# A hybrid attention, retention and pooling backbone: retention in its own queue, pooling in place, and a reordered opening

## The chip, the cores and the metric

The kernel runs on one core of a Trainium2 chip. Its time is the device time of one execution in microseconds; the profile is one execution of its own. PE is the matrix engine (TensorE), DVE the VectorE, ACT the ScalarE, POOL the GpSimd, and SP the SyncE, which here issues DMAs. Each engine works through its own instructions in the order in which the program wrote them, and semaphores hold an instruction back until what it needs is there.

## The reference

Two layers run over 256 latent tokens and 256 context tokens of width 1024, all in float32. The second layer carries the latent tokens on alone; its context tokens only give keys and values.

- Every layer: `u = modulate(rmsnorm(h)) @ w_in`, split into the inputs of three mixers and three gates. The modulation is `silu(c) @ w_ada + b_ada` (adaLN).
- Neighbourhood attention (8 heads of 64): latent queries see a window of the 4 x 64 grid with a bias, and all context keys, in one softmax; context queries see the context.
- Retention (4 heads, keys of 64, values of 128), both directions: `o = ((q k^T) * decay) v`, then a normalization of every head over its 128 values, times `silu(g) * gn_g`.
- Pooling: four groups of 128 channels with windows of 2, 4, 8 and 16 tokens: `(mean over the window - u) @ pool_w * pool_scale`.
- Merge: `(sig(ga)*(a@wpa) + sig(gb)*(r@wpb) + sig(gc)*(p@wpc)) @ w_out`, a gated residual, then a second modulated norm, SwiGLU of hidden width 2816, and a gated residual. A final RMSNorm ends it.

## The kernel before

Every product of float32 operands is made of three matmuls: operands are split into a rounded high part and the rest (`hi`, `lo`), and PE adds `wh*xh + wl*xh + wh*xl` in one PSUM bank (`mm3`, L194 to L198). Activations lie with channels on the partitions and tokens (512, or 256 latent ones) along the row. Weights stream from HBM in 276 chunks of 128 x 1024 (`raw`), and ACT and DVE split each into `hl` (L124, L113) up to three chunks ahead of its use.

PSUM has eight banks under four tags: `pg` (4, products of the projections), `pS` (2, scores), `pT` (1, transposes) and `pO` (1). A tile of a tag waits until the bank that was freed first has been read.

`start()` is the opening. It loads the vectors (`vec`) and the eight tiles of h, computes the norm of h (eight squares into `sq`, summed into `acc`, then summed over partitions by L499, the reciprocal root by `norm_rstd`, and a broadcast by L290), spreads silu(c) over all partitions (L480 on PE, `spread`, L483, copies it into `cb`), and makes the first modulation from adaLN weights in their natural layout: `nat_first` (L459, sixteen matmuls of a chunk `wn`), `nat_copy` and `nat_second` (L469). Its loop over eight chunks then makes seven of the first eight key and query products; the weights of the eighth are kept in `w7` and used behind the loop (L548). Its tiles lie in a pool of their own (`st`), which is closed at its end; the pool of the first mixer (`mx0`) then takes the same place.

`mixer(l, ...)` is the attention, retention and pooling of one layer (L568 to L1052). The order of PE's work around the change is written out in its last part (L829 to L855 and L1035 to L1052): keys and queries, the token-major V (`tokmajor`, CV), retention keys, retention queries, pooling inputs u, the token-major retention values (CRV), the gate products (CG), then the branches A (attention), C (pooling) and B (retention). A branch has four pairs of output chunks; each pair takes two gate products, whose sigmoid (L1000) frees their banks, and two branch products.

The small work of the mixers is woven into these products by lanes. A lane is a list of Python generators; each `next` emits a few instructions and yields. `tick()` (L153) advances the first generator of each of the lanes `pool`, `rope` and `attn` by one step; a generator that is exhausted leaves the list at its next step. `fm` calls `tick` for every two block products of 512 columns or four of 256, and `tokmajor` for every two of 512. `drain(name)` runs what is left of a lane at once. On every second tick DVE's part of the weight splits and, by a rate, adaLN sums (`ada_units`, L385) are emitted too. `pipeline(items, stride)` runs items of several stages staggered, two ticks a stage: first what runs on ACT, DVE and POOL, then PE's part.

The attention's lane has 16 latent items (and 8 context ones in layer 0), one after the other by one stage. The retention's generators are put into the same lane after the gate products: `ret_stack` splits its keys and queries (`rkd`, `rkl`, `rqs`), `ret_item` makes the decay tables of a head (L897 to L906), scores, product with v (L941) and statistics, and `ret_fin` normalizes (L970), transposes (L977) and multiplies by the gate (L980). The decay tables of head 0 are emitted ahead of them, and the four Silu of the gates (L1044) behind. `drain("attn")` ahead of branch B runs what is left.

`pool_task` is the pooling's lane: for each of the four groups POOL adds shifted rows (L803) and corrects the borders (L812), four steps pass, DVE subtracts (L820) into a tile `pl` of the tag `t2`, which it shares with the attention's probabilities, four more steps later PE multiplies (L780) into a `pg` bank, and one step later ACT writes the scaled result over u (L784). `st["hold"]` is 1 while `tokmajor(CRV)` holds all four `pg` banks; the subtractions wait for its end.

Of the kernel before, what the change touches and what calls it, by code (L numbers as in the profile page):

```python
# [8 lines left out]
F32 = mybir.dt.float32  # L9
# [9 lines left out]
KT = 8  # L19
# [13 lines left out]
def hybrid_dit_kernel(ctx: ExitStack, tc: tile.TileContext, hT, wst, adaf, adan, vec_d,  # L33
# [52 lines left out]
        return vec[:, l * V_L + off + i:l * V_L + off + i + 1]  # L86

    raw_t, hl_t = {}, {}
    st = {"dma": 0, "prep": 0, "half": 0, "credit": 0.0, "rate": 0.0, "cap": 10 ** 6, "hold": 0, "lazy": False}
    total = 2 * NCH  # L90

    def raw_tile():
# [46 lines left out]
        load_to(i + 5)  # L139
        flush()  # L140

    lanes = {"attn": [], "pool": [], "rope": []}
    ada_q = []

    def step(q):
        while q:
            try:
                next(q[0])
                break
            except StopIteration:  # L150
                q.pop(0)

    def tick():  # L153
        step(lanes["pool"])
        step(lanes["rope"])
        step(lanes["attn"])
        if st["half"] == 0:
            prep_lo()
            st["credit"] += st["rate"]
            while ada_q and st["credit"] >= 1:  # L160
                ada_q.pop(0)()
                st["credit"] -= 1
        st["half"] ^= 1
# [195 lines left out]
    def new_acc():  # L359
        return sm.tile([128, 512], F32, name="acc", tag="acc", bufs=1)  # L360
# [62 lines left out]

    def start():
        with tc.tile_pool(name="st", bufs=1) as sp:
            nc.scalar.dma_start(out=vec, in_=vec_d)
            h_tiles()
            P.memset(ones, 1.0)
            P.memset(eps, 1e-6)
            make_identity(nc, ident)  # L430
            csil = sp.tile([128, 8, 32], F32, name="csil")
            P.memset(csil, 0.0)
            S.activation(tiny(1, "dummy"), eps, AF.Silu)

            acc = new_acc()
# [5 lines left out]
            st["w7"] = w7 = sp.tile([128, 2, 8, 128], F32R, name="w7")  # L441
            wn = {}

            def nat_load(k):
                if k < KT:
                    wn[k] = sp.tile([128, 8, 256], F32, name="wn", tag="wn", bufs=3)
                    nc.sync.dma_start(out=wn[k], in_=adan[k])

            for k in range(3):
                nat_load(k)  # L450
                load_to(k)

            outs = [pg() for _ in range(4)] + [pS(), pS(), pT(), pO()]
            nat = outs[7]

# [26 lines left out]
            def spread(i):  # L482
                S.copy(cb[i // 2][:, (i % 2) * 512:(i % 2) * 512 + 512], outs[i])  # L483

            for k in range(KT):
                t = sp.tile([128, 512], F32, name="sq", tag="sq", bufs=4)
                if k in (2, 5):
                    V.tensor_tensor(t, h[k], h[k], op=ALU.mult)
                else:
                    S.activation(t, h[k], AF.Square)  # L490
                if k == 0:
                    V.tensor_copy(acc, t)
                else:
# [12 lines left out]
            Rs = sp.tile([128, 512], F32, name="Rs")  # L506
# [61 lines left out]
    def mixer(l, mp, outs, u):  # L568
# [204 lines left out]
        def pool_task():  # L773
            pw = sm.tile([128, 4, 128], F32, name="pw", tag="acc", bufs=1)
            nc.sync.dma_start(out=pw, in_=pw_d[l])
            late = {}

            def pmm(gi, o2):
                pp = pg()
                TE.matmul(pp[:, :nq], pw[:, gi], o2[:, :nq], start=True, stop=True)  # L780
                return pp

            def pev(gi, pp):
                S.activation(up[gi][:, :, 8:264], pp[:, :nq].rearrange("p (s t) -> p s t", t=256), AF.Copy,  # L784
                             scale=vcol(l, V_PS, gi))

            t = [0]

            def pause():
                t[0] += 1  # L790
                if t[0] in late:
                    gi, o2 = late.pop(t[0])
                    pp = pmm(gi, o2)
                    late[-t[0] - 1] = (gi, pp)
                elif -t[0] in late:
                    pev(*late.pop(-t[0]))

            for gi in range(4):
                b = mp.tile([128, 1 + so, 272], F32, name="pb", tag="pb", bufs=1)
                a, w = up[gi], 1  # L800
                for j in range(gi + 1):
                    n = 272 - 2 * w + 1
                    P.tensor_tensor(b[:, :, :n], a[:, :, :n], a[:, :, w:w + n], op=ALU.add)  # L803
                    a = b
                    w *= 2
                    yield
                    pause()
                s0 = 8 - w // 2
# [13 lines left out]
                late[t[0] + 4] = (gi, o2)  # L822
                yield
                pause()
            while late:
                yield
                pause()

        if both:  # L829
            for i in range(8):  # L830
                if i == 4:
                    prep_to(10)
                (ev_nak(i) if i < 4 else ev_naq(i - 4))(outs[i])
        else:
            for i, o in enumerate(outs):
                ev_nak(i)(o)
            n = len(outs)
            fm([(chunk8(base + CK + i), ev_nak(i)) for i in range(n, 4)], hn, ALL)
            fm([(chunk8(base + CQ + i), ev_naq(i)) for i in range(4)], hn, cq)
        if both:  # L840
            decay_logs(u)
        st["lazy"] = True
        lanes["attn"].append(pipeline(items, 1, (10 if both else 0)))
        tokmajor(base + CV, hn, nav)
        fm([(chunk8(base + CRK + i), ev_k(i)) for i in range(2)], hn, ALL)
        fm([(chunk8(base + CRQ + i), ev_q(i)) for i in range(2)], hn, cq)
        fm([(chunk8(base + CU + i), ev_u(i)) for i in range(4)], hn, cq)
        drain("rope")
        lanes["pool"].append(pool_task())
        st["hold"] = 1  # L850
        tokmajor(base + CRV, hn, rv)
        st["hold"] = 0
        fm([(chunk8(base + CG + i), ev_g(i)) for i in range(4)], hn, cq)
        drain("attn")
        st["lazy"] = False  # L855

        m = [mp.tile([128, 512], F32, name=f"m{i}", tag=f"nak{i}") for i in range(4)] + nav
# [106 lines left out]
        def ret_fin(hd):  # L964
# [17 lines left out]

            return [(None, None), (norm, None), (None, trans), (fin, None)]

        def msplit(ks):
            for k in ks:
                split([t[:, cq] for t in hn[k]], m[k][:, cl])
# [60 lines left out]
        drain("attn")  # L1048
        branch(base + CB, [gt[i] for i in range(4)], False, True)
        if both:  # L1050
            h_tiles()
# [298 lines left out]
```

## Time and profile before

| | us |
|---|---|
| median of 3 runs | 1366.77 |
| fastest and slowest run | 1366.04, 1368.06 |
| the profiled execution | 1367.57 |
| span of the profiled execution, first to last instruction | 1365.8 |
| PE busy | 1326.2 |
| PE loading weights | 1151.9 |
| DVE busy | 847.6 |
| ACT busy | 580.7 |
| POOL busy | 152.7 |

The mean granted clock of PE in the span was 0.987 of full speed. A busy time says how long an engine had an instruction at work; matmuls overlap at their ends, so PE's is not the time that its multiplications need. L12 is line 12 of the kernel as printed. A wait is the idle time of an engine ahead of an instruction, put down to what released it last. A row of a timeline gives the start in us from the start of the span, the duration, the engine, line and operation, what is written and read, the shape, a count of merged instructions and, in brackets, the idle time ahead.

### The profile page before, as it was taken

The numbers are of one execution on the slowest core, as the hardware profiler recorded it, in microseconds if no ns is written. First come the engines' busy times: TensorE is split into PE (matmuls) and PEld (weight loads), VectorE is DVE, ScalarE is ACT, GpSimd is POOL, SyncE is SP. The second block draws the span as 40 slices with busy tenths as digits, with TensorE's granted clock in tenths as the row PEclk, the third lists the DMA queues.
The fourth block names the chain that finished last, engine by engine and source line by source line (L and its number), as shares of the span: only waits on it lengthen the run. The fifth ranks groups of instructions, "written<-read, shape, count | busy, mean of one in ns | idle before, by whom it ended". The sixth has DMA issues, their size and how long they took to land.

```text
span 1365.8 us, 20012 instructions
## 1 busy us (share of the span) xinstructions
PE 1326.2 (97%) x7842; PEld 1151.9 (84%) x7842; DVE 847.6 (62%) x1454; ACT 580.7 (43%) x907; POOL 152.7 (11%) x213
## 2 busy tenths in 40 slices
PE   7999999899999999999999999999999999999997
PEld 5777777788888898888888888988889999899997
DVE  4566452877877666566565654676438877655554
ACT  4455555452232444232123232456466545643453
POOL 0034113211000010000000000232134200000000
PEclk8999999999999999999999999999999999999998
DMA  8433312343544514454445652143336665455552
GB/s 301 164 99 132 104 63 92 124 137 126 169 170 163 192 62 154 139 170 158 149 140 186 212 171 87 61 159 108 131 124 197 223 239 185 140 185 198 181 176 95
DMA packets 61150, 207.28 MB, mean 152 GB/s; under 512 B 6912, under 2 KB 11392, under 8 KB 60032
## 3 DMA queue, kind: packets, MB, share of 16 engines
q1 hardware_dynamic: 49392, 163.96, 35.8%
q10 hardware_dynamic: 11664, 42.04, 9.1%
q8 instruction: 62, 1.02, 0.3%
q14 instruction: 32, 0.26, 0.1%
HBM read 204.93 MB, written 1.05 MB: 151 GB/s over the span
## 4 chain that ended last, share of the span: by engine, by line
PE 89%; DVE 6%; ACT 3%; issue 1%; DMA 1%; POOL 0%; DVEq 0%; ACTq 0%; SPq 0%; POOLq 0%
PE pg L196 26%; PE pg L197 26%; PE pg L198 26%; PE po L941 1%; PE po L687 1%; PE pt L675 1%; DVE hl L113 1%; PE po L459 1%; PE ps L643 1%; PE ps L644 1%; DVE nakl L628 1%; DMA bm<-in_bias 1%; DVE rkl L876 0%; DVE naq L638 0%; DVE acc L494 0%
## 5 line engine op out<-in xcount | busy, mean ns | idle before, releaser
L196 PE MATMUL pg<-hh,hl 128*128 128x256 f32 (+1 forms) x1568 | 528.1, 337 | 2.5 <-ACT tmp L1000 1.4
L197 PE MATMUL pg<-hh,hl 128*128 128x256 f32 (+1 forms) x1568 | 522.9, 333 | 1.4 <-DVE hl L113 1.4
L198 PE MATMUL pg<-hl,hl 128*128 128x256 f32 (+1 forms) x1568 | 523.3, 334 | 0.6 <-POOL hl L326 0.5
L113 DVE TENSOR_TENSOR hl<-raw,hl 128x1024 fp32r<-128x1024 f32 (+1 forms) x276 | 341.4, 1241 | 172.2 <-ACT hl L124 166.9
L124 ACT CAST hl<-raw 128x1024 fp32r<-128x1024 f32 (+1 forms) x276 | 286.9, 1043 | 211.4 <-PE pg L198 112.3
L196 PEld LDWEIGHTS pg<-hh,hl 128*128 128x128 f32 x1568 | 299.7, 191 | 36.1 <-issue 3.8
L197 PEld LDWEIGHTS pg<-hh,hl 128*128 128x128 f32 x1568 | 299.6, 191 | 31.1 <-DVE hl L113 2.1
L198 PEld LDWEIGHTS pg<-hl,hl 128*128 128x128 f32 x1568 | 299.2, 191 | 30.6 <-POOL hl L326 1.4
L385 DVE CUSTOM_DVE_ANT_0 tmp<-ada,cb 128x1024 bf16<-128x1024 f32 x128 | 156.1, 1226 | 26.7 <-DMA ada<-in_adaf 17.3
L196 PE MATMUL pg<-fh,hl 128*128 128x256 f32 (+1 forms) x374 | 121.6, 325 | 0.0
L197 PE MATMUL pg<-fh,hl 128*128 128x256 f32 (+1 forms) x374 | 121.4, 325 | 0.0
L198 PE MATMUL pg<-fl,hl 128*128 128x256 f32 (+1 forms) x374 | 121.4, 325 | 0.0
L326 POOL TENSOR_TENSOR hl<-tmp,hh 128x256 fp32r<-128x256 f32 x20 | 14.8, 739 | 626.3 <-ACT hh L315 371.1
L298 ACT CAST fh<-sg 128x512 fp32r<-128x512 f32 (+1 forms) x44 | 22.6, 513 | 141.0 <-DVE sg L1150 141.0
L196 PEld LDWEIGHTS pg<-fh,hl 128*128 128x128 f32 x374 | 70.1, 187 | 7.2
L198 PEld LDWEIGHTS pg<-fl,hl 128*128 128x128 f32 x374 | 70.1, 187 | 7.2
L197 PEld LDWEIGHTS pg<-fh,hl 128*128 128x128 f32 x374 | 70.1, 188 | 7.1
L342 DVE SCALAR_TENSOR_TENSOR h<-pg,mods,h 128x256 f32<-128x256 f32 x72 | 32.7, 479 | 65.6 <-PE pg L198 65.4
L1150 DVE TENSOR_TENSOR sg<-pg,sg 128x512 f32<-128x512 f32 (+1 forms) x44 | 24.5, 556 | 51.2 <-PE pg L198 47.8
L1000 ACT ACTIVATE tmp<-pg 128x512 f32<-128x512 f32 (+1 forms) x48 | 23.5, 490 | 76.4 <-PE pg L198 75.2
L196 PE MATMUL pg<-hl,hh 128*128 128x512 f32 x128 | 50.8, 397 | 1.7 <-DVE nakl L628 1.7
L1147 ACT ACTIVATE sg<-pg 128x512 f32<-128x512 f32 (+1 forms) x44 | 21.6, 490 | 68.4 <-PE pg L198 68.4
(248 smaller groups left out, 1555.7 us busy)
## 6 DMA issues: line engine op xcount, KB each, us to landing
raw<-in_wst SPq DMA_DIRECT2D x276, 512.0 KB, 3.8
ada<-in_adaf ACTq DMA_DIRECT2D x80, 512.0 KB, 4.2
wn<-in_adan SPq DMA_DIRECT2D x8, 1024.0 KB, 7.4
h<-in_hT SPq DMA_DIRECT2D x16, 256.0 KB, 5.5
bm<-in_bias SPq DMA_DIRECT2D x32, 128.0 KB, 2.1
out<-yt SPq DMA_DIRECT2D x4, 256.0 KB, 3.2
cs<-in_rope SPq DMA_DIRECT2D x2, 256.0 KB, 3.1
pw<-in_pw SPq DMA_DIRECT2D x2, 256.0 KB, 3.8
```

Of the source, the lines that this page charges most:

```text
L113: V.tensor_tensor(a[:, 1], r[:, b], a[:, 0].bitcast(F32), op=ALU.subtract)
L124: S.copy(a[:, 0], r[:, b])
L196: TE.matmul(o, wh, xh, start=a, stop=False)
L197: TE.matmul(o, wl, xh, start=False, stop=False)
L198: TE.matmul(o, wh, xl, start=False, stop=z)
L298: S.copy(d0, src)
L326: P.tensor_tensor(hn[k][1][:, c], t[:, c], hi, op=ALU.subtract)
L342: V.scalar_tensor_tensor(h[k][:, c], o, mods[l][:, col + k, s:s + 1], h[k][:, c], op0=ALU.mult, op1=ALU.add)
L385: V.tensor_tensor_reduce(out=tmp().bitcast(BF16), in0=tiles[n], in1=cb[s], scale=1.0, scalar=0.0, op0=ALU.mult, op1=ALU.add, accum_out=mod ...
L1000: S.activation(sg[f][:, cl], o, AF.Sigmoid)
L1147: S.activation(e["s"][:, c], o, AF.Silu)
L1150: V.tensor_tensor(e["s"][:, c], o, e["s"][:, c], op=ALU.mult)
```

## The change

The opening: `vec` is loaded by SP, ahead of h; the memset of `ones`, the first table load and the allocation and loads of the first chunks come in another order; `w7` is allocated between the second and third `wn`; ACT makes all eight squares; the copies `spread(0)` to `spread(3)` stand behind the squares and the norm's sums; `nat_first(0)` stands ahead of the norm's broadcast.

The mixer: retention gets a lane `ret`, which `tick` advances only when the lane `attn` is empty. Its generator is put in ahead of `tokmajor(CRV)`, and its parts run in the order of before, with two waits: for `hold` ahead of the heads, and for `gated` (set once the four Silu are emitted) ahead of the final part. Pooling writes the difference over u, with two steps between POOL's work and DVE's; the hold stands behind all four differences, and then the four matmuls and their evictions alternate, one a step.

```diff
-    lanes = {"attn": [], "pool": [], "rope": []}
+    lanes = {"attn": [], "pool": [], "rope": [], "ret": []}
...
-        step(lanes["attn"])
+        step(lanes["attn"] or lanes["ret"])
...
-            nc.scalar.dma_start(out=vec, in_=vec_d)
+            nc.sync.dma_start(out=vec, in_=vec_d)
             h_tiles()
-            P.memset(ones, 1.0)
             P.memset(eps, 1e-6)
             make_identity(nc, ident)
+            P.memset(ones, 1.0)
+            S.activation(tiny(1, "dummy"), eps, AF.Silu)
...
+            for k in range(3):
+                nat_load(k)
+                load_to(k)
+                if k == 1:
+                    st["w7"] = w7 = sp.tile([128, 2, 8, 128], F32R, name="w7")
+
             csil = sp.tile([128, 8, 32], F32, name="csil")
             P.memset(csil, 0.0)
...
-                if k in (2, 5):
-                    V.tensor_tensor(t, h[k], h[k], op=ALU.mult)
-                else:
-                    S.activation(t, h[k], AF.Square)
+                S.activation(t, h[k], AF.Square)
...
-                if k in (3, 4, 6):
-                    spread(max(k - 3, 0) - (k > 4))
+            spread(0)
+            spread(1)
             o = outs[4]
             for i in range(4):
                 TE.matmul(o[:, i:i + 1], acc[:, i * 128:(i + 1) * 128], ones[:, 0:1], start=True, stop=True)
+            nat_first(0)
             y = norm_rstd(o, 4)
+            spread(2)
             spread(3)
             R = norm_bcast(y, range(4), outs[6])
-            nat_first(0)
             t0 = nat_copy()
...
         def pool_task():
             pw = sm.tile([128, 4, 128], F32, name="pw", tag="acc", bufs=1)
             nc.sync.dma_start(out=pw, in_=pw_d[l])
+            ov = [t[:, :, 8:264] for t in up]
...
-                for _ in range(4):
-                    yield
-                    pause()
-                while st["hold"]:
-                    yield
-                o2 = t2("pl")
-                ov = o2[:, :nq].rearrange("p (s t) -> p s t", t=256)
-                V.scalar_tensor_tensor(ov, b[:, :, s0:s0 + 256], 1.0 / w, up[gi][:, :, 8:264],
+                yield
+                yield
+                V.scalar_tensor_tensor(ov[gi], b[:, :, s0:s0 + 256], 1.0 / w, ov[gi],
                                        op0=ALU.mult, op1=ALU.subtract)
-                late[t[0] + 4] = (gi, o2)
                 yield
-                pause()
-            while late:
+            while st["hold"]:
                 yield
-                pause()
+            for gi in range(4):
+                pp = pmm(gi)
+                yield
+                pev(gi, pp)
+                yield
...
+        def ret_lane():
+            items = [ret_item(hd) for hd in range(4)]
+            items[0][0][0]()
+            items[0][1][0]()
+            items[0][0] = items[0][1] = (None, None)
+            yield
+            yield from ret_stack()
+            while st["hold"]:
+                yield
+            yield from pipeline(items, 4 if both else 2)
+            while not st["gated"]:
+                yield
+            yield from pipeline([ret_fin(hd) for hd in range(4)], 2)
...
         lanes["pool"].append(pool_task())
         st["hold"] = 1
+        lanes["ret"].append(ret_lane())
         tokmajor(base + CRV, hn, rv)
         st["hold"] = 0
         fm([(chunk8(base + CG + i), ev_g(i)) for i in range(4)], hn, cq)
         drain("attn")
+        for i in range(4):
+            S.activation(gt[i], gt[i], AF.Silu)
+        st["gated"] = True
         st["lazy"] = False
...
-        items = [ret_item(hd) for hd in range(4)]
-        items[0][0][0]()
-        items[0][1][0]()
-        items[0][0] = items[0][1] = (None, None)
-        lanes["attn"].append(ret_stack())
-        lanes["attn"].append(pipeline(items, 4 if both else 2))
-        lanes["attn"].append(pipeline([ret_fin(hd) for hd in range(4)], 2))
         st["rate"] = 0.75 if both else 0.45
-        for i in range(4):
-            S.activation(gt[i], gt[i], AF.Silu)
         branch(base + CA, None, True)
         drain("pool")
         branch(base + CC, [up[i][:, :, 8:264] for i in range(4)], False)
-        drain("attn")
+        drain("ret")
+        st["gated"] = False
         branch(base + CB, [gt[i] for i in range(4)], False, True)
```

## Rows read from the trace of the kernel before

**Rows 1.** The page, busy us of each engine, share of the span, instructions.
```profile
PE 1326.2 (97%) x7842; PEld 1151.9 (84%) x7842; DVE 847.6 (62%) x1454; ACT 580.7 (43%) x907; POOL 152.7 (11%) x213
```

**Rows 2.** Waits of PE: who waited <- for whom, us in total, times, longest.
```profile
PE pt L290 <- DVE rstd L266: 3.8, 3, 1.3
PE pg L780 <- DVE pl L820: 3.5, 1, 3.5
PE pt L977 <- DVE y L970: 3.2, 1, 3.2
PE pg L196 <- ACT tmp L1000: 3.1, 4, 1.1
PE po L941 <- DVE sm L923: 1.8, 1, 1.8
PE pg L196 <- DVE nakl L628: 1.7, 1, 1.7
```

**Rows 3.** Three stretches: length, busy (count) of PE, PEld, DVE, ACT, POOL, PEclk, DMA.
```profile
12.60:26.20 13.60, 10.17 (x56) 6.83 (x57) 5.90 (x16) 5.01 (x10) 0.00 (x0) 0.50 0.86 333
251.50:254.90 3.40, 3.40 (x10) 2.63 (x9) 3.40 (x6) 0.59 (x1) 0.00 (x0) 0.50 0.74 240
1101.50:1104.90 3.40, 2.97 (x14) 2.98 (x15) 2.74 (x9) 1.76 (x3) 0.00 (x0) 0.51 0.28 114
```

**Rows 4.** Timeline of the opening, ACT, DVE and PE, to the first dense matmul.
```profile
6.00 1.72 ACT L490 ACTIVATE sq<-h 128x512 f32<-128x512 f32 x3
...
7.18 0.69 DVE L494 TENSOR_TENSOR acc<-acc,sq 128x512 f32<-128x512 f32 x1
...
7.79 0.68 DVE L488 TENSOR_TENSOR sq<-h 128x512 f32<-128x512 f32 x1
...
8.50 2.29 DVE L494 TENSOR_TENSOR acc<-acc,sq 128x512 f32<-128x512 f32 x3
...
10.72 0.63 ACT L490 ACTIVATE sq<-h 128x512 f32<-128x512 f32 x1 [0.30 <-DMA h<-in_hT]
...
13.77 1.86 PE L499 MATMUL ps<-ones,acc 128*128 128x1 f32 x8 [3.19 <-DVE acc L494]
16.85 2.07 PE L290 MATMUL pt<-ident,rstd 128*128 128x128 f32 x8 [1.22 <-DVE rstd L266]
18.86 1.94 PE L459 MATMUL po<-wn,csil 128*32 128x256 f32 x16
21.34 1.01 PE L469 MATMUL po<-sel,wt 128*128 128x2 f32 x4 [0.55 <-DVE wt L463]
...
24.71 0.80 PE L196 MATMUL pg<-hh,hl 128*128 128x512 f32 x1
```

**Rows 5.** Timeline of POOL and DVE where the first mixer begins.
```profile
80.24 0.56 POOL L610 MEMSET bm<- 128x256 f32 x2 [78.50 <-PE po L198]
80.32 5.66 DVE L628 TENSOR_TENSOR nakl<-pg,nakd 64x512 fp32r<-64x512 f32 x8 [7.80 <-PE po L198]
```

**Rows 6.** Timeline of DVE in layer 0's branch A, the fourth subtraction.
```profile
249.44 0.69 DVE L820 SCALAR_TENSOR_TENSOR pl<-pb,up 128x512 f32<-128x512 f32 x1
```

**Rows 7.** Two stretches of layer 1, its gate products and its branches, columns as in rows 3.
```profile
998.80:1010.80 12.00, 12.00 (x101) 11.95 (x100) 6.05 (x7) 5.95 (x9) 1.01 (x1) 1.00 0.41 135
...
1040.00:1110.00 70.00, 64.98 (x539) 64.52 (x538) 57.78 (x112) 39.48 (x61) 14.35 (x18) 0.98 0.63 213
```

**Rows 8.** Timeline of ACT where layer 1's branch A opens.
```profile
1015.40 1.24 ACT L871 CAST rkd<-rk 64x512 fp32r<-64x512 f32 x2
```

**Rows 9.** Timeline of DVE and POOL in layer 1's attention.
```profile
957.28 1.03 DVE L670 TENSOR_SCALAR p<-p,rs 128x512 f32<-128x512 f32 x1
957.29 0.74 POOL L655 TENSOR_TENSOR bm<-bm,mask 128x256 f32<-128x256 f32 x1 [2.13 <-DVE rs L669]
...
963.41 0.49 DVE L670 TENSOR_SCALAR p<-p,rs 128x512 f32<-128x512 f32 x1
```

**Rows 10.** The pooling tile pb from 100 us on: length, DVE and POOL busy (count).
```profile
100.00:1365.00 1265.00, 4.42 (x8) 30.76 (x44) 0.99 0.45 149
```

More of the change, by code (lines that the diff above doesn't have):

```diff
@@ L88, in hybrid_dit_kernel @@
     raw_t, hl_t = {}, {}
-    st = {"dma": 0, "prep": 0, "half": 0, "credit": 0.0, "rate": 0.0, "cap": 10 ** 6, "hold": 0, "lazy": False}
+    st = {"dma": 0, "prep": 0, "half": 0, "credit": 0.0, "rate": 0.0, "cap": 10 ** 6, "hold": 0, "gated": False, "lazy": False}
     total = 2 * NCH
@@ L425, in start, with nat_load @@
         with tc.tile_pool(name="st", bufs=1) as sp:
-            nc.scalar.dma_start(out=vec, in_=vec_d)
+            nc.sync.dma_start(out=vec, in_=vec_d)
             h_tiles()
-            P.memset(ones, 1.0)
             P.memset(eps, 1e-6)
             make_identity(nc, ident)
+            P.memset(ones, 1.0)
+            S.activation(tiny(1, "dummy"), eps, AF.Silu)
+            acc = new_acc()
+            wn = {}
+            def nat_load(k):
+                if k < KT:
+                    wn[k] = sp.tile([128, 8, 256], F32, name="wn", tag=f"wn{k % 3}")
+                    nc.sync.dma_start(out=wn[k], in_=adan[k])
+            for k in range(3):
[3 more added lines that the diff above has]
+                    st["w7"] = w7 = sp.tile([128, 2, 8, 128], F32R, name="w7")
             csil = sp.tile([128, 8, 32], F32, name="csil")
             P.memset(csil, 0.0)
-            S.activation(tiny(1, "dummy"), eps, AF.Silu)
-            acc = new_acc()
             gb = sp.tile([128, 8], F32, name="gb")
@@ L440, in start @@
                                    op0=ALU.add, op1=ALU.mult)
[L441 to L451, printed above, removed]
             outs = [pg() for _ in range(4)] + [pS(), pS(), pT(), pO()]
@@ L775, in pool_task, with pmm @@
             nc.sync.dma_start(out=pw, in_=pw_d[l])
-            late = {}
-            def pmm(gi, o2):
+            ov = [t[:, :, 8:264] for t in up]
+            def pmm(gi):
                 pp = pg()
-                TE.matmul(pp[:, :nq], pw[:, gi], o2[:, :nq], start=True, stop=True)
+                TE.matmul(pp[:, :nq], pw[:, gi], ov[gi], start=True, stop=True)
                 return pp
             def pev(gi, pp):
-                S.activation(up[gi][:, :, 8:264], pp[:, :nq].rearrange("p (s t) -> p s t", t=256), AF.Copy,
+                S.activation(ov[gi], pp[:, :nq].rearrange("p (s t) -> p s t", t=256), AF.Copy,
                              scale=vcol(l, V_PS, gi))
[L787 to L796, printed above, removed]
             for gi in range(4):
@@ L812, in pool_task @@
                         P.tensor_tensor(b[:, s, c], b[:, s, c], icnt[:, gi, e], op=ALU.mult)
-                for _ in range(4):
-                    yield
-                    pause()
-                while st["hold"]:
-                    yield
-                o2 = t2("pl")
-                ov = o2[:, :nq].rearrange("p (s t) -> p s t", t=256)
-                V.scalar_tensor_tensor(ov, b[:, :, s0:s0 + 256], 1.0 / w, up[gi][:, :, 8:264],
+                yield
+                yield
+                V.scalar_tensor_tensor(ov[gi], b[:, :, s0:s0 + 256], 1.0 / w, ov[gi],
                                        op0=ALU.mult, op1=ALU.subtract)
-                late[t[0] + 4] = (gi, o2)
                 yield
-                pause()
-            while late:
+            while st["hold"]:
                 yield
[L827 to L853, printed above, removed]
-        drain("attn")
-        st["lazy"] = False
-        m = [mp.tile([128, 512], F32, name=f"m{i}", tag=f"nak{i}") for i in range(4)] + nav
+            for gi in range(4):
[3 more added lines that the diff above has]
+                yield
         tts = range(4) if both else range(2, 4)
@@ L983, in ret_fin @@
             return [(None, None), (norm, None), (None, trans), (fin, None)]
+        def ret_lane():
[11 more added lines that the diff above has]
+            yield from pipeline([ret_fin(hd) for hd in range(4)], 2)
+        if both:
+            for i in range(8):
+                if i == 4:
+                    prep_to(10)
+                (ev_nak(i) if i < 4 else ev_naq(i - 4))(outs[i])
+        else:
+            for i, o in enumerate(outs):
+                ev_nak(i)(o)
+            n = len(outs)
+            fm([(chunk8(base + CK + i), ev_nak(i)) for i in range(n, 4)], hn, ALL)
+            fm([(chunk8(base + CQ + i), ev_naq(i)) for i in range(4)], hn, cq)
+        if both:
+            decay_logs(u)
+        st["lazy"] = True
+        lanes["attn"].append(pipeline(items, 1, (10 if both else 0)))
+        tokmajor(base + CV, hn, nav)
+        fm([(chunk8(base + CRK + i), ev_k(i)) for i in range(2)], hn, ALL)
+        fm([(chunk8(base + CRQ + i), ev_q(i)) for i in range(2)], hn, cq)
+        fm([(chunk8(base + CU + i), ev_u(i)) for i in range(4)], hn, cq)
+        drain("rope")
+        lanes["pool"].append(pool_task())
+        st["hold"] = 1
+        lanes["ret"].append(ret_lane())
+        tokmajor(base + CRV, hn, rv)
+        st["hold"] = 0
+        fm([(chunk8(base + CG + i), ev_g(i)) for i in range(4)], hn, cq)
+        drain("attn")
+        for i in range(4):
+            S.activation(gt[i], gt[i], AF.Silu)
+        st["gated"] = True
+        st["lazy"] = False
+        m = [mp.tile([128, 512], F32, name=f"m{i}", tag=f"nak{i}") for i in range(4)] + nav
         def msplit(ks):
```

1 line of the change is left out of this document (removed).

## The prediction

> **What bounds the kernel now.** I read the page's busy line first, then the waits of the matmul engine (PE), then the granted clock behind the long waits, then the timelines around each. PE is busy for 1326.2 of 1365.8 us [rows 1], and the change gives it the same multiplications, so what can be won is PE's idle time, 39.6 us, and matmuls run at the lower clock. Of the idle time, 3.5 us stand before a pooled matmul (L780), 3.2 before a transpose of the retention (L977), 3.1 in four waits for a sigmoid (L1000), 1.8 before a retention product (L941) and 3.8 before three L290 [rows 2]; the opening has 3.2 more, before L499 [rows 4]. Behind L780's and L977's waits, and through most of the opening, the granted clock is 0.50: 1.2 instead of 2.4 GHz [rows 3].
>
> **Part 1, the opening.** PE reaches the sums of squares (L499) at 13.77 and its first dense matmul (L196) at 24.71 [rows 4].
> Squares: DVE made two of the eight itself (0.68 us each) and seven additions (2.29 us for three, 0.69 for one: a pitch of 0.80). Now ACT makes all squares, at 0.57 each (1.72 for three), and two of the three cb copies (L483) between them go behind the last one. DVE keeps one copy and seven additions, the first at 7.18: 7.18 + 6 * 0.80 + 0.69 = 12.7. The last square began at 10.72, when its h tile had landed, and takes 0.63; one addition later is 12.1. So L499 comes at about 12.5: 1.3 us won [rows 4]. The load of vec goes from ACT's queue to the head of SP's, so every h tile is issued one issue later, and the last is waited for: a loss of at most an issue, 0.4, or a gain as large where vec lands sooner. I take 0. wn, raw and pw keep their order on SP; the memset of csil moves on a POOL that has nothing else.
> nat_first(0): PE waited 1.22 us for the norm (16.85), ran the broadcast (2.07) and nat_first (1.94), and the copy behind it ended before L469 at 21.34 [rows 4]. Now nat_first stands ahead of the broadcast, and the 1.22 us pass under it. From the end of L499 to L469 it was 21.34 - 15.63 = 5.7; it becomes 1.94 + 2.07 = 4.0, with the copy under the broadcast: 1.7 won. No row shows when its weights (wn) landed, only that they had by 18.86; if no sooner, this 1.7 is lost.
> Together 3.0. The clock rose at 26.2, 1.5 us into the dense matmuls. If it rises no sooner although these start at 21.7, 4.5 us run at 1.2 GHz in place of 1.5, and 1.5 is lost. Bounds 1.0 to 4.0.
> The kept weights (w7) at another place of the pool: the mixer's first operations on POOL and on DVE both start at 80.2 to 80.3, behind the last matmul that reads w7 [rows 5]. POOL's writes bm, which by the tiles' sizes begins 64.5 KB into the new pool, where the old one was 45 KB long: the wait is for the whole pool, not for an address. Moving w7 inside it changes nothing, and the 1.7 us for L628 [rows 2] stay. Bounds: 0 to 1.7 won.
>
> **Part 2, layer 0.** A step (tick) of the lanes comes with every six 512-column matmuls; from the V product to the end of the gate products there are 16 + 8 + 8 + 16 + 16 + 16 = 80. The attention lane needs 10 + 2 * 34 = 78 and leaves its list at step 79, so the retention's queue opens at step 80 of 80: only its first decay tables move, three exponentials, to where ACT waits for PE. ret_stack starts at step 81 as before.
> Pooling does move. Without the hold its subtractions are issued at steps 52, 57, 63 and 70 and its matmuls at 71, 73, 75 and 77, all in the gate stage. Before, the fourth subtraction (L820) stood on DVE behind the splits of rkl and rqs and two adaLN sums, ran at 249.44 [rows 6], and PE had stopped for it: 3.5 us, with 3.4 us at 1.2 GHz behind them [rows 3], half of which, 1.7, is lost. Won: 5.2. The new wait: a subtraction now stands two steps behind its POOL operations instead of four or more, and behind it on DVE stand softmax and weight splits (L113). POOL has little else there; I take 0 and a lower bound of 3.5. Next late would be rqs on DVE, but the first scores need head 0's alone, the first of the four. Writing in place costs nothing and frees a t2 buffer.
>
> **Part 3, layer 1.** Here a step is twelve 256-column matmuls (six of 512 for V and k): 16 + 8 + 4 + 8 + 16 + 8 = 60 up to the end of the gate products, and the attention needs 1 + 2 * 26 = 53. The queue opens at step 55; before, it opened at 61. Counting on through ret_stack (9 steps), the four heads (26) and the finals, the finals' transposes stood at steps 101, 105, 109 and 113 and now stand at 97, 101, 105 and 109. Branch C ends at 108. Before, the drain ran two of the four with no other matmul between them, through one PSUM bank, each behind DVE's L980 and L970; now only the last, whose operand is made at step 106. So the 3.2 us go [rows 2], and with them a stretch at 1.2 GHz with 2.97 us of matmuls [rows 3], half of it 1.5. Sum 4.7; bounds 2 to 5.
> The 1.8 us before L941 [rows 2]: the third head stood on steps 84 to 87, beside the split for branch C and the fourth head's decay tables. Now the fourth head stands there and no tables come with it. I take 1.5; bounds 0 to 1.8.
> The sigmoid waits, 3.1 us [rows 2], fall where branch A opens with exponentials, Silu, rkd, rqs and two table loads on ACT. Exponentials and rkd (1.24 us for two of four [rows 8]) now stand in the gate stage, where ACT is busy for 5.95 and DVE for 6.05 of 12 us [rows 7]. Silu, both table loads, rqs and three of the four pooled evictions stay in the opening, and the first branch product still needs the bank of the first sigmoid. I take 1.9; bounds 0 to 3.1.
> Layer 1: 4.7 + 1.5 + 1.9 = 8.1; bounds 2 to 10.
>
> **Sum.** 3.0 + 5.2 + 8.1 = 16.3 us. The profiled execution took 1367.57 us around its span of 1365.8, with 1.8 outside, unchanged: 1367.57 - 16.3 = 1351.3. The median of the runs, 1366.77, lies 0.8 lower; that is inside what I can tell, and I do not shift it.
>
> **A rule that speaks against it.** Beside a POOL operation that began in the same moment, a DVE scaling (L670) took 1.03 us instead of 0.49 [rows 9]. The Trainium skill, page "SBUF — State Buffer", section "Who interferes with whom", says that DVE and GpSimd share a port pair: where a DVE instruction uses two ports, or has two SBUF inputs while GpSimd reads, the later of the two is blocked for the whole of the other. This pair of rows agrees. By the rule the moved pooling is no free filling but a price on DVE, which is the third rival.
>
> **Rivals.** One: layer 1 gives nearly nothing. DVE is busy for 57.8 of 70 us in its branches [rows 7]; without PE's waits the same DVE and ACT work has less time, and waits for weights or sigmoids of the same sum could come. Against it: the work that moves goes where both engines are half idle. Time: 1367.57 - 3.0 - 5.2 = 1359.4.
> Two: w7's move does release the mixer's first operations, since its last reader ends both waits [rows 5]. Against it: bm. Time: 1351.3 - 1.7 = 1349.6.
> Three, slower: POOL blocks DVE beside the attention's tail. Pooling's POOL operations are 30.8 us in all [rows 10]. If they stand beside softmax and L113, and DVE's delay goes on into transposes and weights, PE waits. To be slower by 0.2% (about what a measurement of this kernel can tell from no change) they must eat 16.3 + 2.7 = 19 us, 62% of the 30.8. For it: the scaling [rows 9]. Against it: POOL works beside the attention already, and [rows 2] show no PE wait for the softmax. With 70%, 21.6 us: 1351.3 + 21.6 = 1372.9.
> Four: no change. The opening wins 1.0, and what layer 0 wins PE loses again in both branch openings, to rqs, sigmoids and weights. Time: 1366.6.
>
> **How the numbers follow.** Forecast 0.60 (its own range 1347 to 1356), rival one 0.17, two 0.08, three 0.07, four 0.08. The range goes from 1346.5 (opening 4.0, layer 0 5.4, layer 1 10, w7 1.7) to 1361.0 (rival one with the opening at 1.4) and leaves out rivals three and four. Faster by over 0.2% are the forecast, one and two: 0.85; same 0.08; slower 0.07.
>
> **What would show it.** Right: L499 near 12.5 and the first L196 near 21.7; the four pooled matmuls of layer 0 ahead of its last gate eviction, with no wait; no wait of 3 us at L977 in layer 1, and no 0.50 clock between the opening and the last layer's second norm; the wait for L628 still there. Wrong: PE waits of over 2 us in layer 1's gate stage or branch A, L113 at 1.7 us and more beside POOL in the V and gate stages, or a first dense matmul later than 23.5.

## The result, and the profile after

The changed kernel takes 1349.08 us (median of 4 runs, 1348.88 to 1350.82); the kernel before, beside it, 1367.41 (1366.04 to 1368.69). The ratio is 0.9868, 95% interval 0.9855 to 0.988: 18 us faster, where 16.3 were forecast. The profiled execution took 1349.18 us around a span of 1347.4, so the time outside the span is 1.8 again.

The page of the changed kernel answers to [rows 1]: busy us of each engine, share, instructions. PE is busy for 5.6 us less with the same 7842 matmuls (fewer of them ran at the lower clock), and idle for 26.8 us instead of 39.6.

```profile
PE 1320.6 (98%) x7842; PEld 1148.0 (85%) x7842; DVE 847.9 (63%) x1452; ACT 583.0 (43%) x909; POOL 146.4 (11%) x213
```

PE's waits in the changed kernel answer to [rows 2]; line numbers have moved by a few.

```profile
PE ps L497 <- DVE acc L492: 3.1, 1, 3.1
PE pg L481 <- ACT csil L476: 3.0, 1, 3.0
PE pt L290 <- DVE rstd L266: 2.6, 2, 1.3
...
PE pg L196 <- DVE nakl L627: 1.7, 1, 1.7
...
PE po L896 <- DVE sm L878: 1.2, 1, 1.2
...
PE pg L196 <- ACT rv L249: 0.8, 1, 0.8
```

Gone are the pooled matmul's 3.5 (L780), the drain's 3.2 (L977) and all 3.1 of the sigmoids (L1000). One L290 went. The wait for nakl is as long as before. New are 0.8 us for the rv copies and, inside the opening, 0.8 us ahead of the first dense matmul (L517, in the timeline below). L896 is the retention product that was L941.

Stretches of the changed kernel (columns as in [rows 3]): two of the opening, one over branch A's opening in layer 0, layer 1's gate products and branches as in [rows 7], and the last layer's second norm.

```profile
11.60:18.40 6.80, 5.99 (x35) 4.70 (x36) 2.06 (x8) 3.13 (x7) 0.00 (x0) 0.50 1.02 425
18.40:21.10 2.70, 1.36 (x19) 0.62 (x19) 2.03 (x6) 1.78 (x4) 0.00 (x0) 1.00 1.00 417
240.00:250.00 10.00, 10.00 (x49) 8.26 (x48) 8.75 (x14) 4.35 (x6) 0.00 (x0) 1.00 0.38 128
990.50:1002.50 12.00, 12.00 (x100) 11.95 (x99) 6.96 (x8) 9.74 (x16) 7.40 (x12) 1.00 0.29 96
1031.00:1092.50 61.50, 60.26 (x512) 60.07 (x512) 51.00 (x99) 35.04 (x54) 10.32 (x15) 1.00 0.67 229
1148.20:1151.60 3.40, 3.40 (x16) 3.26 (x17) 3.03 (x8) 3.13 (x8) 1.48 (x2) 0.50 0.00 0
```

The clock is at 0.50 only in the opening, for 3.4 us at the last layer's second norm (6.8 before), and at the very end. In layer 1's gate stage ACT went from 5.95 to 9.74 us of 12 and POOL from 1.01 to 7.40, with PE full: that is the work that left the branches.

The opening of the changed kernel, timeline of ACT, DVE and PE, answers to [rows 4].

```profile
9.28 3.08 DVE L492 TENSOR_TENSOR acc<-acc,sq 128x512 f32<-128x512 f32 x4 [0.26 <-ACT sq L488]
10.88 0.63 ACT L488 ACTIVATE sq<-h 128x512 f32<-128x512 f32 x1 [0.31 <-DMA h<-in_hT]
...
12.41 1.87 PE L497 MATMUL ps<-ones,acc 128*128 128x1 f32 x8 [3.11 <-DVE acc L492]
14.21 1.93 PE L460 MATMUL po<-wn,csil 128*32 128x256 f32 x16
...
16.07 2.08 PE L290 MATMUL pt<-ident,rstd 128*128 128x128 f32 x8
...
17.94 0.73 PE L470 MATMUL po<-sel,wt 128*128 128x2 f32 x4
...
19.25 1.07 PE L460 MATMUL po<-wn,csil 128*32 128x256 f32 x16 [0.57 <-DVE mods L473]
...
21.08 0.50 PE L196 MATMUL pg<-hh,hl 128*128 128x512 f32 x1 [0.77 <-ACT hh L517]
```

nat_first (L460) now fills the time before L290, which waits for nothing. The second L460 takes 1.07 us where the first took 1.93: the clock rose at 18.4, ahead of the dense matmuls and not behind their start.

**Where the 18 us came from.** Both profiles hold the same 6882 dense matmuls (L196 to L198) in the same order, so the n-th of one is the same product as the n-th of the other, and the difference of their starts is what has been won up to there. Read at the stage borders, and for the experiments too (us won in the stage; "norm" is the last layer's second norm):

| stage | forecast | changed | opening alone | pooling alone | retention alone | tables alone | all but pooling |
|---|---|---|---|---|---|---|---|
| opening | 3.0 | 4.0 | 3.0 | -0.7 | 0.8 | 0.0 | 2.1 |
| layer 0 | 5.2 | 4.2 | -0.6 | 2.8 | 4.4 | 4.4 | 4.4 |
| layer 1 | 8.1 | 9.2 | 0.1 | -3.1 | 9.5 | 0.2 | 9.6 |
| norm | 0 | 0.5 | 0 | -0.5 | 0 | -0.3 | -0.4 |

The columns behind the forecast are single executions, all against the one profile of before. That profile was 0.3 to 0.5 us slower than each of them in the V stage, which stands in every column's layer 0. The half clock behind one wait differs between executions by 3.4 us of stretch, so differences of 1 us between columns say little, and in the opening row those of 2.

### The profile page after: what moved, and what is told of

Same layout as the page of the kernel before. It is cut to its first block, busy times and chain, and to the rows that moved or that the text cites. A ratio compares the mean times of both kernels' runs of the same rounds, so it can differ in the third digit from the quotient of the medians.

```text
span 1347.4 us, 20009 instructions
## 1 busy us (share of the span) xinstructions
PE 1320.6 (98%) x7842; PEld 1148.0 (85%) x7842; DVE 847.9 (63%) x1452; ACT 583.0 (43%) x909; POOL 146.4 (11%) x213
## 4 chain that ended last, share of the span: by engine, by line
PE 89%; DVE 5%; ACT 4%; issue 1%; DMA 1%; SPq 0%; ACTq 0%; DVEq 0%
PE pg L196 27%; PE pg L197 27%; PE pg L198 27%; PE pt L674 1%; PE po L686 1%; PE po L896 1%; ACT hl L124 1%; DVE hl L113 1%; PE ps L642 1%; PE ps L643 1%; PE po L460 1%; DVE tmp L385 1%; DMA raw<-in_wst 0%; DMA h<-in_hT 0%; ACT hh L317 0%
## 5 line engine op out<-in xcount | busy, mean ns | idle before, releaser
L196 PE MATMUL pg<-hh,hl 128*128 128x256 f32 (+1 forms) x1568 | 526.4, 336 | 2.7 <-ACT hh L317 1.1
L198 PE MATMUL pg<-hl,hl 128*128 128x256 f32 (+1 forms) x1568 | 522.0, 333 | 0.6 <-POOL hl L326 0.5
L196 PEld LDWEIGHTS pg<-hh,hl 128*128 128x128 f32 x1568 | 298.3, 190 | 35.8 <-issue 3.8
L198 PEld LDWEIGHTS pg<-hl,hl 128*128 128x128 f32 x1568 | 298.2, 190 | 30.6 <-POOL hl L326 1.4
L196 PE MATMUL pg<-fh,hl 128*128 128x256 f32 (+1 forms) x374 | 121.6, 325 | 0.0
L198 PE MATMUL pg<-fl,hl 128*128 128x256 f32 (+1 forms) x374 | 121.4, 325 | 0.0
L196 PEld LDWEIGHTS pg<-fh,hl 128*128 128x128 f32 x374 | 70.1, 187 | 7.1
L198 PEld LDWEIGHTS pg<-fl,hl 128*128 128x128 f32 x374 | 70.1, 187 | 7.1
L196 PE MATMUL pg<-hl,hh 128*128 128x512 f32 x128 | 50.9, 397 | 1.7 <-DVE nakl L627 1.7
```

What stands on the lines that cost most here:

```text
L196: TE.matmul(o, wh, xh, start=a, stop=False)
L198: TE.matmul(o, wh, xl, start=False, stop=z)
```

## The experiments

**The three parts, each alone on the kernel before.** Only the opening:

```diff
 (start() of the changed kernel, everything else as before)
-            nc.scalar.dma_start(out=vec, in_=vec_d)
+            nc.sync.dma_start(out=vec, in_=vec_d)
...
+            nat_first(0)
             y = norm_rstd(o, 4)
```

> Only the opening of the change, on the kernel before. The first dense matmul of the opening came 3.6 us earlier in the changed kernel and the end of the opening 4.05 us earlier. If the opening's gain stands on its own, this kernel takes 1367.4 - 4.0 = 1363.4 us, and the waits at L780 (3.5), L977 (3.2) and L1000 (3.1) of before are all still there. Rival, the prediction's 3.0 with the extra 1.0 borrowed from a later stage: 1364.4.

Measured: 1365.52 us against 1367.65, ratio 0.9981 (0.9971 to 0.999): 2.6 us, between 1.4 and 4.0. The waits of the layers are all as before. Its own profile shows 3.0 won, and 0.6 given back in layer 0, where the same 3.5 us wait had 6.8 us of half clock behind it instead of 3.4.

Only the pooling:

```diff
-                while st["hold"]:
-                    yield
-                o2 = t2("pl")
...
+                V.scalar_tensor_tensor(ov[gi], b[:, :, s0:s0 + 256], 1.0 / w, ov[gi],
```

> Only the pooling of the change (difference in place, no hold ahead of it), on the kernel before. Theory, each part pays for its own wait: L780's wait of 3.5 goes with the 1.7 us of its half clock, a new wait of 0.8 to 1.0 us for the rv copies (L249) comes, because POOL's fourth window stands beside two softmax scalings; layer 1 keeps the 3.2 at L977. 1367.4 - 4.3 = 1363.1, and 1 to 2 us less if the pooling also is what filled the time of the sigmoids (L1000). Rival, the sigmoid waits of 3.1 us are the pooling's alone: 1360.

Measured: 1367.83 against 1367.65, ratio 0.9994 (0.9985 to 1.0003): nothing. Both expectations were wrong. PE's waits of this kernel:

```profile
PE pt L962 <- DVE y L955: 3.2, 1, 3.2
PE po L926 <- DVE sm L908: 2.9, 1, 2.9
PE pg L196 <- ACT tmp L985: 2.0, 1, 2.0
...
PE ps L897 <- DVE sm L908: 1.7, 1, 1.7
...
PE pg L196 <- ACT rv L249: 0.8, 1, 0.8
```

The wait for the pooled matmul is gone in layer 0, and four sigmoid waits have become one. But in layer 1 the retention, still at its old place, now makes PE wait 2.9 and 1.7 us for its scores on DVE. And there are three stretches at half clock in layer 1 where the kernel before had one (length, busy (count) of PE, PEld, DVE, ACT, POOL, PEclk, DMA):

```profile
1018.30:1021.80 3.50, 3.50 (x19) 3.50 (x18) 1.59 (x4) 3.45 (x6) 1.16 (x2) 0.51 0.78 287
1059.30:1066.10 6.80, 6.08 (x28) 6.11 (x29) 4.76 (x10) 6.74 (x12) 1.00 (x1) 0.50 0.52 172
1103.70:1107.10 3.40, 3.40 (x18) 3.40 (x18) 3.32 (x6) 1.31 (x2) 0.00 (x0) 0.50 0.03 12
```

In this execution, of 1368.14 us, layer 1 loses 3.1 us and eats what layer 0 won. The eleven runs go from 1365.49 to 1368.69, five of them under 1366.5 at a slightly higher granted clock (0.988 to 0.990 instead of 0.985 to 0.987), so the loss need not be 3.1 in each. Why the scores come later once the pooling has gone was not tried.

Only the retention's queue:

```diff
-        step(lanes["attn"])
+        step(lanes["attn"] or lanes["ret"])
...
 (ret_lane() as in the changed kernel; pool_task() and start() as before)
```

> Only the retention's own queue, on the kernel before, with the pooling as it was. Theory: the wait at L780 (3.5, and its half clock at 251) stays; in layer 1 the 3.2 at L977 go with their half clock (4.9 by the two traces), and the sigmoid waits go too, since the exponentials and rkd leave the opening of branch A: 1367.4 - 4.9 - 3 to 4.3 = 1358.2 to 1359.5. Rival, only the drain is the retention's and the sigmoid waits are the pooling's: 1362.5.

Measured: 1352.91 against 1367.65, ratio 0.9888 (0.9873 to 0.9903): 15.3 us. The time is 5.3 to 6.6 us below the theory's and 9.6 below the rival's. By the profiles this one edit wins 13.9 us in the two layers, where the whole change wins 13.4; by the times its 15.3 and the 2.6 of the opening alone make 17.9 of the 18 us. The surprise is layer 0, where L780 was to wait 3.5 as before. PE's waits of this kernel:

```profile
PE pg L780 <- DVE pl L820: 1.2, 1, 1.2
...
PE po L912 <- DVE sm L894: 0.9, 1, 0.9
...
PE pg L196 <- ACT tmp L1018: 0.4, 2, 0.3
```

**Which part of the retention does that?** In layer 0 only the first head's decay tables change place. So the next kernel is the one before with that alone; PE's order of instructions is exactly that of before.

```diff
 (retention alone, and:)
             yield
+            while not st["gated"]:
+                yield
             yield from ret_stack()
-            while st["hold"]:
-                yield
```

> The kernel before with one thing moved: the decay tables of the first retention head (three exponentials on ACT, 1.7 us) stand one gate copy earlier in layer 0, and before the last gate copies in layer 1; everything else of the retention keeps its place, and PE's order is that of before. Theory: in layer 0 ACT's chain Silu, rkd, weight copies ran 1.7 us late behind the three, and DVE's fourth pooled difference with it; L780's wait falls from 3.5 to about 1.2 and the half clock behind it goes, 4.0 us, as with the whole queue alone; the drain's 3.2 at L977 stay. 1367.6 - 4.0 = 1363.6, and up to 3 less if the tables also held up layer 1's sigmoids (waits of 3.1). Rival, the prediction's: tables moved into idle ACT time are worth nothing, L780 still waits 3.5: 1367.6.

Measured: 1361.66 against 1368.23, ratio 0.995 (0.9937 to 0.9962): 6.8 us. ACT of this kernel, timeline where layer 0's gate stage ends (start, us):

```profile
225.46 0.72 ACT L874 ACTIVATE dm<-dtab,lg 128x384 f32<-128x384 f32 x1
226.07 0.70 ACT L875 ACTIVATE tmp<-dtab,lg 128x384 f32<-128x384 f32 x1
226.67 0.52 ACT L876 ACTIVATE dm<-dm 128x384 f32<-128x384 f32 x1
228.92 0.59 ACT L619 COPY gt<-pg 128x512 f32<-128x512 f32 x1 [1.73 <-PE pg L198]
229.53 1.28 ACT L998 ACT_TABLE_LOAD   x1
```

The tables end at 227.2, in time in which ACT then still waits 1.73 us for PE's last gate product. Before, they stood behind that copy, and Silu, rkd, rqs and the weight copies stood behind them. DVE's queue waits for those copies, and the fourth pooled difference stands in it:

```profile
246.64 0.69 DVE L820 SCALAR_TENSOR_TENSOR pl<-pb,up 128x512 f32<-128x512 f32 x1
```

Before it was 249.44 [rows 6], 2.8 us later, though PE had been only 0.5 behind. PE's waits of the same kernel:

```profile
PE pt L948 <- DVE y L941: 3.2, 1, 3.2
...
PE po L912 <- DVE sm L894: 1.8, 1, 1.8
PE pg L196 <- ACT tmp L1018: 1.8, 3, 0.6
...
PE pg L780 <- DVE pl L820: 1.2, 1, 1.2
```

L780's wait falls from 3.5 to 1.2, and no half clock follows it. The sigmoid waits fall from 3.1 to 1.8. The drain's 3.2 stay: these need the queue's earlier opening. The theory is confirmed for layer 0, and the prediction's zero refuted. In layer 1 this execution wins only 0.2 us, although the sigmoid waits are shorter, since it holds a stretch at half clock that the kernel before did not have:

```profile
1057.00:1060.40 3.40, 3.40 (x19) 3.40 (x18) 1.98 (x5) 3.38 (x9) 1.01 (x1) 0.50 0.61 181
```

**The pooling taken out of the changed kernel:**

```diff
 (the changed kernel with pool_task() as before)
+                while st["hold"]:
+                    yield
+                o2 = t2("pl")
```

> The changed kernel with the pooling put back as before (own buffer, held differences). Theory, the retention's queue does the work and the pooling's move adds next to nothing beside it (it takes off 1.2 at L780 and adds 0.8 at the rv copies): 1349.1 + 0 to 0.7 = 1349.5. Rival, the prediction's, pooling carries layer 0's gain of 5.2: 1354.3.

Measured: 1351.18, ratio to before 0.9877 (0.9862 to 0.9893). The changed kernel gave 0.9868 (0.9855 to 0.988) and, timed again beside the last two kernels below, 1350.62 and 0.9881 (0.9861 to 0.99). These overlap. By stages, layers 0 and 1 win 4.4 and 9.6 without the pooling's move, 4.2 and 9.2 with it. So beside the retention's queue the pooling is worth nothing that these runs can tell; where the profile of this kernel is behind, it is in the opening and in the last norm, whose instructions are the same.

> The changed kernel itself, timed once more beside the two below, to see how far its opening goes with the execution: 1349.1, with the sums of squares (L497) anywhere from 12.4 to 13.5 as in the runs so far that have this opening.

The time, 1350.62, is 1.5 us above the one named, with ratios that overlap; L497 came at 13.84, a little outside the span named. The square of h's fourth tile waited for its load here, 2.40 us (ACT, timeline):

```profile
9.24 3.27 ACT L488 ACTIVATE sq<-h 128x512 f32<-128x512 f32 x5 [2.40 <-DMA h<-in_hT]
```

**The new wait, 0.8 us at L249.** DVE of the changed kernel in layer 0's gate stage, a pair of softmax scalings alone, then a pair and a small scaling beside POOL:

```profile
183.33 0.62 DVE L721 TENSOR_SCALAR p<-p,rs 128x256 f32<-128x256 f32 x2
...
191.82 1.63 DVE L721 TENSOR_SCALAR p<-p,rs 128x256 f32<-128x256 f32 x2
193.37 0.68 DVE L709 TENSOR_REDUCE mx<-ps 128x2 f32<-128x512 f32 x1
194.09 0.61 DVE L710 TENSOR_SCALAR mx<-mx 128x2 f32<-128x2 f32 x1
```

POOL of the same kernel, the fourth window's additions:

```profile
191.06 3.62 POOL L791 TENSOR_TENSOR pb<-pb 128x538 f32<-128x538 f32 x3
```

```diff
-                    P.tensor_tensor(b[:, :, :n], a[:, :, :n], a[:, :, w:w + n], op=ALU.add)
+                    if not (both and gi == 3 and j):
+                        P.tensor_tensor(b[:, :, :n], a[:, :, :n], a[:, :, w:w + n], op=ALU.add)
```

> The changed kernel without three of the four additions of the fourth window on POOL in layer 0 (3.6 us of POOL left out, so the output of that window is not the reference's). Theory, POOL's additions held DVE's softmax scaling (two at 1.63 us in place of 0.61, and 0.61 in place of 0.17), and through softmax and ACT's rv copies PE: the scalings take 0.35 each, the 0.8 us wait at L249 is gone. Rival, ACT's own weight copy ahead of the rv copies makes that wait: it stays at 0.8.

Measured in one execution, 1348.67 us. DVE at the same two places:

```profile
192.76 0.62 DVE L721 TENSOR_SCALAR p<-p,rs 128x256 f32<-128x256 f32 x2
...
194.01 0.17 DVE L710 TENSOR_SCALAR mx<-mx 128x2 f32<-128x2 f32 x1
```

The scalings are short again, the rv copies start behind an earlier softmax, and PE has no wait at L249, though ACT's weight copy still stands ahead of the rv copies: the rival is out. Nor has the kernel with the pooling as before a wait there. From the V stage to the middle of the gate stage this kernel loses 0.0 us where the changed kernel loses 1.1. The time itself moves less, since this execution's opening was 1.1 us behind the other's. The rows confirm the theory.

**nat_first(0) behind the broadcast again:**

```diff
-            nat_first(0)
             y = norm_rstd(o, 4)
...
             R = norm_bcast(y, range(4), outs[6])
+            nat_first(0)
```

> The changed kernel with the first adaLN products (nat_first(0)) behind the broadcast of the norm again. Theory, the prediction's 1.7: PE waits 1.2 to 1.3 us at L290 once more, the first dense matmul comes 1.7 us later, at 22.8; if that pause also keeps the clock at half until 24 to 26, another 1 to 2 us go: 1349.1 + 1.7 to 3.5. Rival, wn is not in by then or the copy is exposed elsewhere and the move is worth nothing: 1349.1.

Measured: 1351.89, ratio to before 0.9879 (0.9865 to 0.9892). That time is 2.8 above the changed kernel's first median and 1.3 above its second, and the three ratios to before overlap, so the times alone do not price the move. The timeline of PE shows what moved:

```profile
13.38 1.87 PE L497 MATMUL ps<-ones,acc 128*128 128x1 f32 x8 [3.64 <-DVE acc L492]
16.47 2.08 PE L290 MATMUL pt<-ident,rstd 128*128 128x128 f32 x8 [1.22 <-DVE rstd L266]
...
20.96 1.01 PE L470 MATMUL po<-sel,wt 128*128 128x2 f32 x4 [0.55 <-DVE wt L464]
...
24.34 0.80 PE L196 MATMUL pg<-hh,hl 128*128 128x512 f32 x1
```

From the end of L497 to L470 it is 5.7 us, in the changed kernel 3.7. The first dense matmul is back at 24.34, and the clock stays at half until 26.1. The squares and vec alone leave only 0.4 of the opening's gain in this execution.

**The wait for nakl, and two kernels made from what was found.** First the changed kernel with one edit:

```diff
-        with tc.tile_pool(name="mx0", bufs=1) as mp:
+        with tc.tile_pool(name="mx0", bufs=1, reuse_waits="tile") as mp:
```

> The changed kernel with one edit: the first mixer's tiles wait for the earlier users of their own bytes, not for the whole pool of the opening. Theory, w7's last reader held DVE and POOL through the whole-pool wait: the memset of bm and the first nakl split (L627) start when the first key product is done, near 68.7 instead of 76.3, PE's 1.7 us for L627 go, 1349.1 - 1.7 = 1347.4. Rival, bank or address holds them anyway (the queries' copies on ACT, L634, are issued behind the same wait): 1349.1.

Measured: 1348.6 (1346.74 to 1349.41), ratio to before 0.9853 (0.984 to 0.9867). The wait at L627 is gone, and 1.9 us are won there: the first product behind the opening starts with no pause. DVE and POOL begin the mixer's work inside the opening (POOL's first nakl memset at 66.71, DVE's split at 74.79, behind ACT's copies and not at 68.7 as expected). The profiled execution, of 1349.41 us, had lost 4 us ahead of that point against the one of the changed kernel: its clock fell to half once more, from 22.4 to 29.2, under dense matmuls. That accounts for this execution's time; the median of the four runs shows no gain beyond the noise either, and what the other three lost is not shown. So the wait was for the whole pool, and w7's new address alone could not shorten it.

Then with the pooling's windows from the widest to the narrowest as well, so that POOL's long additions stand beside earlier heads:

```diff
-            for gi in range(4):
+            for gi in (3, 2, 1, 0):
                 b = mp.tile([128, 1 + so, 272], F32, name="pb", tag="pb", bufs=1)
```

> The changed kernel with two edits: tile-wise waits for the first mixer (takes off the 1.7 to 1.9 at L627), and the pooling's windows taken from the widest to the narrowest, so that the widest no longer stands beside the last softmax scalings (takes off the 0.8 to 1.0 at L249). Theory: 1349.1 - 2.8 = 1346.3. Rival: the widest window blocks the softmax at its new place and PE waits there instead, only L627's part is won: 1347.3.

Measured: 1346.49 (1346.32 to 1346.81), ratio to before 0.9854 (0.9835 to 0.9872); the changed kernel beside it 1350.62 (1348.78 to 1351.52), every run of it slower. The waits at L627 and L249 are both gone. This version beats both kernels, by 4.1 us against the changed one where 2.8 were expected; the order of the windows was not timed alone.

> The same with vec's load on ACT's queue again, as before. In the runs with vec ahead of the h tiles on one queue the fourth square began at 7.7 to 8.9, before at 7.75 to 7.96. Theory: the fourth square comes at 7.9 again, the other four follow at 0.66 each, L497 comes at about 12.0 instead of 13.1, and csil's later 4.3 costs nothing since its products end before that: 1.1 less than the kernel with the two edits. Rival: a later csil moves the eight products and cb copies into the squares on ACT and nothing is won, or 1 us is lost.

```diff
-            nc.sync.dma_start(out=vec, in_=vec_d)
+            nc.scalar.dma_start(out=vec, in_=vec_d)
```

Measured: 1346.1 (1345.81 to 1346.78), ratio 0.9851 (0.9833 to 0.987): no difference from the one above that these runs can tell. The square of h's fourth tile came at 7.66 without waiting for its load, but L497 at 12.81, not 12.0: now DVE's seven additions, at a pitch of 0.80 without a pause, end last. (The expectation's 7.75 to 7.96 for before are the third tile's, on DVE; the fourth tile's square began at 7.1 to 7.3 there, on ACT.)

```profile
6.09 3.21 ACT L488 ACTIVATE sq<-h 128x512 f32<-128x512 f32 x6
7.28 5.47 DVE L492 TENSOR_TENSOR acc<-acc,sq 128x512 f32<-128x512 f32 x7
...
12.81 1.12 PE L497 MATMUL ps<-ones,acc 128*128 128x1 f32 x8 [1.68 <-DVE acc L492]
```

## Why the prediction was right, and which of its steps were not

The total was 2.2 us short (1351.3 forecast, 1349.08 measured) and inside the forecast's own range. That it is so near is in part luck: the profile shown won 1.0 us more in the opening than forecast and 1.0 less in layer 0, and layer 0's gain was put down to the pooling alone, which beside the retention's queue is worth nothing that the runs can tell.

- **Opening, 3.0.** 4.0 in the profile shown, the best of seven; 3.0, 2.1, 2.9, 0.05, 2.6 and 3.4 in six others with this opening, 2.6 in the time of the opening alone. nat_first's 1.7 is confirmed (2.0 from L497's end to L470, and no pause). The squares' 1.3 is too large: L497 starts at 13.1 in the mean of eight profiles with the new squares (12.41 to 13.84) against 13.8 of four with the old, 0.7. The 12.41 of the profile shown, so near the 12.5 named, is the earliest of the eight, which is luck. Two steps were off. One is vec at "I take 0", with a loss of 0.4 at most: with vec at the head of SP's queue the square of h's fourth tile waited for its load and began at 7.7 to 9.2, and the last square at 10.9 to 11.9; with vec on ACT's queue they began at 7.1 to 7.7, right behind the one ahead, and at 10.5 to 10.8. The other is the 12.5 itself: the prediction's own sum for DVE's additions is 12.7, and with vec back on ACT's queue, where nothing else holds them, L497 came at 12.81. Since the additions then end last, moving vec back won nothing that the runs can tell. The clock went to either side: it rose at 18.4 in the profile shown, for good only at 29.2 in the worst.
- **w7, 0.** Right, and for the reason given: only when the tiles no longer waited for the whole pool did the wait go.
- **Layer 0, 5.2.** 4.2. L780's wait and its half clock went, as forecast. The step that failed is the retention's: "only its first decay tables move, three exponentials, to where ACT waits for PE". What moves was right; its price was taken as nothing, and by the tables alone it is 4.0 us (the table's 4.4 less the V stage's 0.4). The three were 1.7 us at the head of a chain ACT to DVE to PE that ended in the very wait that the forecast put on the pooling alone. Either edit breaks the chain: with the pooling alone the wait is gone, with the tables alone 1.2 of its 3.5 us are left. So the two don't add.
- **The new wait, "I take 0 and a lower bound of 3.5".** It came, 0.8 to 1.0 us, by the third rival's mechanism: a DVE scaling beside a POOL addition took up to 1.24 us instead of 0.35. The Trainium skill, page "SBUF — State Buffer", section "Who interferes with whom", says that where a DVE instruction such as a scaling uses two ports, the later of it and a GpSimd instruction is blocked for all of the other. These rows agree: the stretched L710 ended at 194.70 and the additions beside it at 194.68, though the records do not always show which of the two came first. It cost a twentieth of the 19 us that this rival needed, since two of the three stretched pairs of layer 0 had no PE wait behind them.
- **Layer 1, 8.1.** 9.2. The drain gave 4.9 by the two profiles (4.7 forecast): as forecast, only the last pair of transposes is left for it, and it waits for nothing (PE of the changed kernel, timeline):

```profile
1085.77 0.38 PE L932 MATMUL pt<-ident,y 128*128 128x128 f32 x2
```

  The sigmoid waits went entirely, 3.1 instead of 1.9: 1.3 with the tables alone, 2.7 with the whole queue. Of the retention product's 1.8 only 0.6 went, not 1.5. Rival one (layer 1 gives nearly nothing) is refuted for the change, but for the pooling alone it holds: its profile even loses 3.1 us there.
- **The norm, 0.5.** Not forecast, and not the change's: timed again, the changed kernel had 6.8 us of half clock there, as before.

## What to carry to other kernels

When a step moves, follow every short operation that leaves the head of another engine's queue, also where no matmul reads it: 1.7 us of exponentials off ACT's queue were worth 4.0 us, most of a pooled matmul's wait and the half clock behind it. Two edits that both cure one wait are not to be added; run each alone before the gain is put down to one. And a filler for POOL is free only where DVE has no scaling beside it that PE will wait for.

## What the runs showed of the hardware

Identical openings differed by 4 us between the profiles of seven executions: the last square began between 10.9 and 11.9, L497 started between 12.4 and 13.8, and the granted clock rose to 1.00 for good between 18.4 and 29.2, in two executions after falling to 0.50 a second time (21.8 to 25.2 and 22.4 to 29.2). Beside POOL's additions, two of DVE's scalings from SBUF to SBUF took 0.47 and 1.24 us instead of 0.35 each, while its reduction from PSUM (L709, 0.68) took what it takes alone.
